# A two-block network in one launch: operands of the first mix in PSUM, scores of the other sign, and GpSimd's weight parts in four pieces

## The chip, the cores and the metric

The kernel runs on one core of one Trainium2 chip. The metric is the device time of one execution in microseconds, as the median of several. The core has a matmul engine (PE), a vector engine (DVE), a scalar engine (ACT), a general engine (GpSimd, POOL in the rows) and a queue engine for transfers (SP).

## The reference, cut to what matters

Two blocks are computed on 256 tokens of width 1024, in float32. The change lies almost wholly in the first mix of the first block:

```python
h = rmsnorm(x, norm1_g[l])
z = h @ w_in[l] + b_in[l]
glu_val, glu_gate, q, k, v, g_conv, g_attn = jnp.split(z, [c0, c1, c2, c3, c4, c5], axis=-1)
conv_out = conformer_conv(glu_val, glu_gate, conv_w[l], conv_b[l], conv_ln_g[l], conv_ln_b[l], w_conv_out[l])
q = rope(q.reshape(B, S, N_Q_HEADS, HEAD_DIM), positions)
k = rope(k.reshape(B, S, N_KV_HEADS, HEAD_DIM), positions)
attn_out = swa_sink_attention(q, k, v, attn_sinks[l]) @ w_attn_o[l]
merged = jax.nn.sigmoid(g_conv) * conv_out + jax.nn.sigmoid(g_attn) * attn_out
x = x + merged @ w_out[l]
```

`conformer_conv` gates, runs a 31-tap convolution over the tokens for each of the 1024 channels, normalises each token over its channels (layernorm), applies SiLU and multiplies by `w_conv_out`. `swa_sink_attention` is attention in a window of 128 tokens over 16 heads, with one learned sink score per head in the softmax (`m = maximum(max(s), sk)`, `e = exp(s - m)`, `p = e / (sum(e) + exp(sk - m))`). Behind it come an expert layer (a projection to keys, a top-16 choice on DVE, gathered rows) and the second block with two mixes and two feed-forward layers.

## The kernel before, in words

Features lie on the 128 partitions and tokens along the free axis, so an activation of one 128-feature chunk is a 128x256 tile. Weights come in tiles of 128x1024, eight blocks of 128x128 each, 279 tiles in all, through a ring of `raw`, `whi` and `wlo` buffers that SP's queue fills. `split_tile` (line 143) makes two parts of a tile: ACT rounds it to `whi` (line 148), and the rest, `wlo = raw - whi`, is made by GpSimd for the 62 tiles in the table `POOL` (line 150) and by DVE for the others (line 152). The 62 are tiles 4 to 51 of the first mix and 14 of the expert layer's 16 query tiles. One output chunk of 128 features is eight blocks with three matmuls each: the high part times the high and the low part of the input, and the low part times the high one (lines 171 to 173). It gathers in a PSUM buffer named `mm`, of which there are four; everything else in PSUM uses four buffers named `ax`.

The first mix is written as a run of chunks, with a `tick` after each one that starts work noted for later (`later(n, fn)`), and a `pump` that issues steps of the convolution until a budget is spent. In order:

- the squares of x are summed (`squares`), `rsqrt` (line 350) makes the scale of each token on DVE with small steps on two columns (lines 357 to 363), and `rows` (line 369) spreads it over all partitions: DVE multiplies the unit matrix by the scale (`dg`, line 373), PE multiplies by ones, ACT copies the result. `normalise` (line 550) forms `h` in SBUF and splits it into `hh` and `hl` (ACT, then DVE's subtraction at line 382). The first four chunks run in fp32 on x before that;
- sixteen chunks make the gated input `u` of the convolution (`gated`); `tables` makes the cosine and sine tables `ct` and `st` on DVE (lines 564 to 582);
- two chunks make keys and values, eight the queries. `rot` (line 676) takes a projection out of PSUM on ACT as `q0`; a chunk later PE swaps the halves (`sw`), and DVE forms `sw*st`, `q0*ct` and their sum (lines 684 to 686);
- sixteen chunks make the two gates. Beside them runs the attention, two heads at a time (`window_pair`): scores on PE, then `soft` (line 713): DVE adds the mask and takes the largest (line 718), changes its sign (line 719), ACT takes the exponentials, DVE forms the reciprocal of the sum, ACT scales; PE transposes and multiplies by the values;
- the convolution has 31 taps for each of eight chunks, two chunks in turn in one `ax` buffer, a DVE step each (line 622); six taps of the last chunk are done by PE. `BUDGET` sets how much of it is issued after each chunk. When `LN0` projections have been issued, the rest is issued, and `mean` (line 758) sums the eight chunks on DVE (`ysum`, lines 760 and 762); PE spreads the mean (line 768), DVE subtracts it, squares are summed, `rsqrt` and `rows` follow, and `silu` gives the input of `w_conv_out`;
- eight chunks each with `w_attn_o`, `w_conv_out` and `w_out` (`residual`, whose low part is made on DVE at line 411).

`rsqrt` and `rows` are also used by all later norms. Line numbers are those of the kernel before; in rows of the changed kernel they are 5 to 8 higher. A scheduler decides the order on each engine from the order of the code; each engine then works through its own instructions in that order and waits where an input is not there.

## Time and profile before

| what | value |
|---|---|
| median of three runs | 1598.98 us (1590.4 to 1600.01) |
| the profiled execution | 1596.75 us, its span 1595.0 us |
| busy over the span: PE, DVE, ACT, GpSimd | 1525.9, 1150.4, 641.4, 512.7 us |
| the first mix's last chunks end, the expert layer's queries begin | about 284 us |
| granted clock of PE, mean | 0.983 |

PE's busy time counts a matmul from its issue to its result, so a busy PE is not always one at its full pace. The first mix takes the first 284 us of the span; from about 400 us on transfers of gathered rows fill the DMA engines.

### The profile page before, as it was taken

To read this page: it belongs to the slowest core of one execution; us is meant where nothing else is said; L and a number is where in the kernel's file an instruction comes from. 1 tells how busy PE (TensorE), PEld (TensorE's weight loads), DVE (VectorE), ACT (ScalarE), POOL (GpSimd) and SP (SyncE) were. 2 spreads that over 40 slices of the span, in tenths; PEclk is the share of its full clock that TensorE was granted. 3 is DMA by queue.
4 is the path that set the end of the run, shared out by engine and by line. 5 is a ranking of instruction groups with operands and counts; after the bars stand their busy time and mean duration, and the time that the engine had idled before them with its cause. 6 is when DMAs were issued, how large, how long until landed. Compare 5 with 4: busy or idle time off the path is not lost.

```text
span 1595.0 us, 29881 instructions
## 1 busy us (share of the span) xinstructions
PE 1525.9 (96%) x11514; PEld 1462.2 (92%) x11514; DVE 1150.4 (72%) x2535; ACT 641.4 (40%) x1378; POOL 512.7 (32%) x407
## 2 busy tenths in 40 slices
PE   8988989889999999799999999999999999999997
PEld 7877889889999999799989999888999998899986
DVE  6998888697989999744444438867777557776655
ACT  4566655442145544000000015556544445655443
POOL 3734541442477787555545501000000030000000
PEclk9999999999999999899999999999999999999999
DMA  5533446746999999999999966734755576465563
GB/s 190 164 101 94 124 130 212 255 157 209 409 409 409 409 409 409 391 408 409 409 409 409 409 232 187 245 120 130 223 185 185 184 193 205 134 192 183 177 190 111
DMA packets 109678, 399.16 MB, mean 250 GB/s; under 512 B 12516, under 2 KB 12931, under 8 KB 109024
## 3 DMA queue, kind: packets, MB, share of 16 engines
q1 hardware_dynamic: 72720, 262.18, 47.9%
q0 software_dynamic: 35232, 130.64, 21.4%
q10 hardware_dynamic: 1584, 4.45, 0.8%
q8 instruction: 90, 1.47, 0.4%
q14 instruction: 52, 0.43, 0.1%
HBM read 395.04 MB, written 6.11 MB: 252 GB/s over the span
## 4 chain that ended last, share of the span: by engine, by line
PE 65%; DMA 17%; DVE 11%; issue 4%; ACT 2%; POOL 1%; SPq 0%; POOLq 0%; DVEq 0%; ACTq 0%
PE mm L1046 17%; DMA row<-vv,idx 14%; PE mm L171 11%; PE mm L173 11%; PE mm L172 11%; PE ax L1154 2%; DVE ax L622 2%; PE mm L239 2%; PE mm L237 2%; PE mm L238 2%; DVE wlo L152 1%; PE ax L1084 1%; DMA wlo<-vv 1%; POOL wlo L150 1%; DMA raw<-vv 1%
## 5 line engine op out<-in xcount | busy, mean ns | idle before, releaser
L148 ACT ACTIVATE whi<-raw 128x1024 fp32r<-128x1024 f32 x275 | 290.1, 1058 | 591.8 <-PE ax L1154 281.9
L152 DVE TENSOR_TENSOR wlo<-raw,whi 128x1024 fp32r<-128x1024 f32 x213 | 260.7, 1226 | 117.6 <-ACT whi L148 113.5
L173 PE MATMUL mm<-xgh,wlo 128*128 128x256 f32 x1064 | 303.0, 285 | 8.3 <-POOL wlo L150 7.6
L171 PE MATMUL mm<-xgh,whi 128*128 128x256 f32 x1064 | 305.2, 287 | 0.5 <-ACT whi L148 0.5
L172 PE MATMUL mm<-xgl,whi 128*128 128x256 f32 x1064 | 302.1, 284 | 2.6 <-DVE xgl L411 2.6
L1655 DVE SCALAR_TENSOR_TENSOR acc<-row,w,acc 128x1024 f32<-128x1024 f32 x94 | 120.7, 1284 | 151.7 <-DMA row<-vv,idx 149.8
L173 PEld LDWEIGHTS mm<-xgh,wlo 128*128 128x128 f32 x1064 | 203.1, 191 | 9.6 <-POOL wlo L150 8.6
L172 PEld LDWEIGHTS mm<-xgl,whi 128*128 128x128 f32 x1064 | 203.1, 191 | 3.0 <-DVE xgl L411 2.8
L171 PEld LDWEIGHTS mm<-xgh,whi 128*128 128x128 f32 x1064 | 203.0, 191 | 2.7 <-issue 1.3
L150 POOL TENSOR_TENSOR wlo<-raw,whi 128x1024 fp32r<-128x1024 f32 x62 | 148.7, 2406 | 127.5 <-ACT whi L148 125.8
L1640 POOL DMA_INDIRECT row<-vv,idx x96 | 124.1, 1292 | 97.4 <-DMA row<-vv,idx 66.4
L1154 PE MATMUL ax<-G,raw 128*128 128x160 f32 x816 | 122.5, 303 | 9.0 <-DMA raw<-vv 9.0
L1154 PEld LDWEIGHTS ax<-G,raw 128*128 128x128 f32 x816 | 115.2, 192 | 9.7 <-DMA raw<-vv 9.6
L1640 POOL DMA_INDIRECT row<-un,idx x96 | 110.8, 1154 | 38.7 <-DVE a L1645 18.2
L1645 DVE CUSTOM_DVE_ANT_0 junk<-row,h 128x1024 f32<-128x1024 f32 x96 | 120.1, 1251 | 0.4
L1046 PE MATMUL mm<-hn,raw 128*128 128x160 f32 x768 | 112.6, 300 | 0.0
L172 PE MATMUL mm<-hl,whi 128*128 128x256 f32 x368 | 106.6, 290 | 2.2 <-DVE hl L382 2.1
L1046 PEld LDWEIGHTS mm<-hn,raw 128*128 128x128 f32 x768 | 106.3, 190 | 0.0
L1154 PE MATMUL ax<-G,whi 128*128 128x160 f32 x624 | 95.4, 303 | 5.1 <-DMA whi<-vv 5.1
L622 DVE SCALAR_TENSOR_TENSOR ax<-u,cw,ax 128x256 f32<-128x256 f32 x227 | 97.3, 481 | 0.6
L1154 PEld LDWEIGHTS ax<-G,whi 128*128 128x128 f32 x624 | 89.1, 193 | 6.0 <-DMA whi<-vv 5.9
L1154 PE MATMUL ax<-G,wlo 128*128 128x160 f32 x608 | 90.2, 300 | 3.1 <-DMA wlo<-vv 3.1
(436 smaller groups left out, 3345.8 us busy)
## 6 DMA issues: line engine op xcount, KB each, us to landing
raw<-wst SPq DMA_DIRECT2D x278, 512.0 KB
raw<-ut SPq DMA_DIRECT2D x48, 512.0 KB
raw<-vv SPq DMA_DIRECT2D x38, 512.0 KB
whi<-ut SPq DMA_DIRECT2D x36, 512.0 KB
wlo<-ut SPq DMA_DIRECT2D x36, 512.0 KB
whi<-vv SPq DMA_DIRECT2D x33, 512.0 KB
wlo<-vv SPq DMA_DIRECT2D x26, 512.0 KB
raw<-vv POOLq DMA_DIRECT2D x13, 512.0 KB
```

Source lines behind the costliest of these rows:

```text
L148: nc.scalar.activation(hi, raw, AF.Copy)
L150: nc.gpsimd.tensor_sub(lo, raw, hi)
L152: self.pin = nc.vector.tensor_sub(lo, raw, hi)
L171: nc.tensor.matmul(pt, w[:, s], xs[0][:, k], start=first, stop=False)
L172: nc.tensor.matmul(pt, w[:, s], xs[1][:, k], start=False, stop=False)
L173: nc.tensor.matmul(pt, lo[:, s], xs[0][:, k], start=False, stop=last)
L622: nc.vector.scalar_tensor_tensor(y[:, c] if k == 30 else ps, u[:, c, k:k + T], cw[:, c, k:k + 1], ps, op0=ALU.mult, op1=ALU.add)
L1046: nc.tensor.matmul(pt, raw[:, k * 128:(k + 1) * 128], hn[:, k, :N], start=(k == 0), stop=(k == C - 1))
L1154: nc.tensor.matmul(acc[d // 2][:, d % 2, :N], raw[:, d * 128:(d + 1) * 128], G(i), start=False, stop=False, skip_group_check=True)
L1640: self.k.nc.gpsimd.indirect_dma_start(t, None, table, bass.IndirectOffsetOnAxis(ap=self.idx[:, s:s + 1], axis=0))
L1645: self.k.nc.vector.tensor_tensor_reduce(junk, row, self.h, 1.0, 0.0, ALU.mult, ALU.add, self.a[:, s:s + 1])
L1655: self.k.nc.vector.scalar_tensor_tensor(self.acc, row, w, self.acc, op0=ALU.mult, op1=ALU.add)
```

## The change

- `BUDGET` and `LN0`: more convolution steps after each chunk of the first stages (4.0 and 2.8 instead of 3.6 and 2.4; a step of a pair counts 0.8), and the layernorm's sum two projections earlier.
- `split_tile`: GpSimd's subtraction of a tile is written as four of 256 columns.
- `rsqrt`: its two small temporaries lie in one `ax` buffer in PSUM, in every norm.
- `rows`: the scaled unit matrix is made by two ACT instructions instead of one of DVE, in every norm.
- the sinks change their sign once at the start; scores are formed with the other sign, so that the smallest is taken and no sign change is left between DVE's and ACT's step; the exponentials scale by -1.
- `normalise`: `h` lies in PSUM.
- `rot`: DVE forms `(pt + bias) * ct` straight from the projection in PSUM, ahead of the swap; the product with `st` stays in PSUM, and the sum reads it there.
- `mean`: the running sum lies in PSUM.

```diff
-BUDGET = (3.6, 2.4, 2.8, 2.6)
+BUDGET = (4.0, 2.8, 2.8, 2.6)
-LN0 = 42
+LN0 = 40
+PIECE = 256
@@ split_tile
-            nc.gpsimd.tensor_sub(lo, raw, hi)
+            for c in range(0, 1024, PIECE):
+                p = slice(c, c + PIECE)
+                nc.gpsimd.tensor_sub(lo[:, p], raw[:, p], hi[:, p])
@@ rsqrt
-        v = self.small.tile([128, n], F32, name="rv", bufs=2)
-        t = self.small.tile([128, n], F32, name="rt", bufs=2)
+        v = self.pp.tile([128, 2 * n], F32, name="ax", bufs=4)
+        v, t = v[:, :n], v[:, n:]
@@ rows
-        nc.vector.tensor_mul(dg, self.ident[:, None, :].to_broadcast([128, 2, 128]),
-                             r[:, :, None].to_broadcast([128, 2, 128]))
+        for tt in range(2):
+            nc.scalar.activation(dg[:, tt], self.ident, AF.Copy, scale=r[:, tt:tt + 1])
@@ first_mix
+        nc.vector.tensor_scalar(snks, snks, -1.0, None, op0=ALU.mult)
@@ normalise
-                h = p1.tile([128, T], F32, name="h", bufs=2)
+                h = self.pp.tile([128, T], F32, name="ax", bufs=4)
@@ rot
+            q1 = p1.tile([128, T], F32, name="q1", bufs=3)
+            nc.vector.scalar_tensor_tensor(q1, pt, bias, ct, op0=ALU.add, op1=ALU.mult)
-                q1 = p1.tile([128, T], F32, name="q1", bufs=2)
-                nc.vector.tensor_mul(q1, sw, st)
-                nc.vector.tensor_mul(q0, q0, ct)
-                nc.vector.tensor_add(dst, q0, q1)
+                nc.vector.tensor_mul(sw, sw, st)
+                nc.vector.tensor_add(dst, sw, q1)
@@ soft
-                    nc.vector.tensor_tensor_reduce(e[:, ks], sp[:, ks], swa[:, ks], 0.125, snk[:, tt:tt + 1], ALU.add, ALU.max, mx[:, tt:tt + 1])
-                nc.vector.tensor_scalar(mx, mx, -1.0, None, op0=ALU.mult)
+                    nc.vector.tensor_tensor_reduce(e[:, ks], sp[:, ks], swa[:, ks], -0.125, snk[:, tt:tt + 1], ALU.add, ALU.min, mx[:, tt:tt + 1])
-                    nc.scalar.activation(e[:, ks], e[:, ks], AF.Exp, bias=mx[:, tt:tt + 1], accum_out=den[:, tt:tt + 1])
-                    nc.scalar.activation(ds[:, tt:tt + 1], snk[:, tt:tt + 1], AF.Exp, bias=mx[:, tt:tt + 1])
+                    nc.scalar.activation(e[:, ks], e[:, ks], AF.Exp, bias=mx[:, tt:tt + 1], scale=-1.0, accum_out=den[:, tt:tt + 1])
+                    nc.scalar.activation(ds[:, tt:tt + 1], snk[:, tt:tt + 1], AF.Exp, bias=mx[:, tt:tt + 1], scale=-1.0)
@@ mean
-            nc.vector.tensor_add(ysum, y[:, 0], y[:, 1])
+            ps = self.pp.tile([128, T], F32, name="ax", bufs=4)
+            nc.vector.tensor_add(ps, y[:, 0], y[:, 1])
             for c in range(2, C):
-                nc.vector.tensor_add(ysum, ysum, y[:, c])
+                nc.vector.tensor_add(ysum if c == C - 1 else ps, ps, y[:, c])
```

DVE's instructions around the first rotation, that of the keys, before the change (`u` is the gated input, `ax<-u,cw,ax` a convolution step):

```order
L642 SCALAR_TENSOR_TENSOR u<-mm,prm,sg 128x256
L622 SCALAR_TENSOR_TENSOR ax<-u,cw,ax 128x256 x11
L684 TENSOR_TENSOR q_817<-ax,st 128x256
L622 SCALAR_TENSOR_TENSOR ax<-u,cw,ax 128x256
L685 TENSOR_TENSOR q_781<-q_781,ct 128x256
L622 SCALAR_TENSOR_TENSOR ax<-u,cw,ax 128x256
L686 TENSOR_TENSOR kT<-q_781,q_817 128x256
L622 SCALAR_TENSOR_TENSOR ax<-u,cw,ax 128x256 x9
```

And the same place on DVE in the changed kernel:

```order
L650 SCALAR_TENSOR_TENSOR u<-mm,prm,sg 128x256
L630 SCALAR_TENSOR_TENSOR ax<-u,cw,ax 128x256 x5
L688 SCALAR_TENSOR_TENSOR q_831<-mm,prm,ct 128x256
L630 SCALAR_TENSOR_TENSOR ax<-u,cw,ax 128x256 x3
L693 TENSOR_TENSOR ax<-ax,st 128x256
L630 SCALAR_TENSOR_TENSOR ax<-u,cw,ax 128x256
L694 TENSOR_TENSOR kT<-ax,q_831 128x256
L630 SCALAR_TENSOR_TENSOR ax<-u,cw,ax 128x256 x7
```

The product with the cosine stands four steps ahead of the one with the sine and reads the projection's `mm` buffer; the last two steps have an operand in `ax`.

DVE's instructions at the end of the convolution before the change (`sga<-sga,mm` takes up a chunk of `w_attn_o`, `y<-ax,y` subtracts the mean):

```order
L622 SCALAR_TENSOR_TENSOR ax<-u,cw,ax 128x256
L815 SCALAR_TENSOR_TENSOR sga<-sga,mm 128x256
L622 SCALAR_TENSOR_TENSOR y<-u,cw,ax 128x256
L815 SCALAR_TENSOR_TENSOR sga<-sga,mm 128x256
L762 TENSOR_TENSOR ysum<-ysum,y 128x256 x2
L815 SCALAR_TENSOR_TENSOR sga<-sga,mm 128x256
L770 SCALAR_TENSOR_TENSOR y<-ax,y 128x256 x4
```

And in the changed kernel:

```order
L823 SCALAR_TENSOR_TENSOR sga<-sga,mm 128x256
L630 SCALAR_TENSOR_TENSOR ax<-u,cw,ax 128x256 x2
L630 SCALAR_TENSOR_TENSOR y<-u,cw,ax 128x256
L770 TENSOR_TENSOR ax<-ax,y 128x256
L770 TENSOR_TENSOR ysum<-ax,y 128x256
L823 SCALAR_TENSOR_TENSOR sga<-sga,mm 128x256
L778 SCALAR_TENSOR_TENSOR y<-ax,y 128x256 x4
```

Before, three chunks of `w_attn_o` are taken up ahead of the subtraction of the mean; in the changed kernel there are four, two of them above the rows shown. On PE the mean's matmul stands behind 73 matmuls of `w_attn_o` before and behind 99 now, of 192.

## Rows read from the trace of the kernel before

**Rows 1.** Busy time per stage: stretch, length, engines, granted clock, DMA share, GB/s.

```profile
core 0: us, PE busy (x) PEld busy (x) DVE busy (x) ACT busy (x) POOL busy (x), PEclk, DMA share, GB/s
60.00:80.00 20.00, 20.00 (x170) 19.95 (x169) 19.12 (x46) 9.24 (x12) 17.57 (x8) 1.00 0.64 202
28.50:73.00 44.50, 38.61 (x302) 37.26 (x301) 43.09 (x87) 23.66 (x30) 31.05 (x14) 0.96 0.49 156
73.00:98.00 25.00, 21.48 (x154) 20.04 (x154) 22.77 (x53) 11.09 (x23) 13.97 (x6) 0.86 0.47 148
98.00:184.00 86.00, 79.82 (x564) 66.57 (x561) 76.93 (x229) 61.86 (x177) 38.34 (x16) 0.96 0.30 93
184.00:206.80 22.80, 21.37 (x182) 21.17 (x181) 22.77 (x50) 10.29 (x13) 17.29 (x8) 1.00 0.53 162
206.80:230.80 24.00, 18.51 (x134) 18.09 (x135) 20.85 (x43) 11.44 (x22) 11.56 (x5) 0.86 0.43 132
230.80:284.00 53.20, 50.44 (x422) 49.85 (x421) 42.19 (x72) 29.35 (x50) 8.78 (x6) 1.00 0.63 200
284.00:346.00 62.00, 53.90 (x429) 52.54 (x428) 50.55 (x248) 27.00 (x62) 33.10 (x29) 0.94 0.63 219
```

**Rows 2.** DVE's groups by form, 0 to 290 us: busy us, mean ns, idle before.

```profile
L622 DVE SCALAR_TENSOR_TENSOR ax<-u,cw,ax 128x256 f32<-128x256 f32 x227 | 97.3, 481 | 0.6
...
L719 DVE TENSOR_SCALAR mx<-mx 128x2 f32<-128x2 f32 x16 | 9.7, 603 | 0.0
L411 DVE SCALAR_TENSOR_TENSOR xgl<-x,prm,xgh 128x256 fp32r<-128x256 f32 x8 | 9.3, 1168 | 2.1 <-ACT xgh L410 2.1
L686 DVE TENSOR_TENSOR qT<-q,q 128x256 f32<-128x256 f32 x8 | 9.2, 1154 | 0.0
L382 DVE TENSOR_TENSOR hl<-h,hh 128x256 fp32r<-128x256 f32 x8 | 8.8, 1139 | 0.0
L685 DVE TENSOR_TENSOR q<-q,ct 128x256 f32<-128x256 f32 x9 | 8.8, 974 | 0.0
...
L762 DVE TENSOR_TENSOR ysum<-ysum,y 128x256 f32<-128x256 f32 x6 | 6.6, 1094 | 0.0
...
L684 DVE TENSOR_TENSOR q<-ax,st 128x256 f32<-128x256 f32 x9 | 3.7, 416 | 1.9 <-PE ax L682 1.9
```

**Rows 3.** GpSimd's timeline, 28 to 62 us: start, length, what.

```profile
37.19 2.39 POOL L150 TENSOR_TENSOR wlo<-raw,whi 128x1024 fp32r<-128x1024 f32 x1 [4.25 <-ACT whi L148]
...
43.94 2.39 POOL L150 TENSOR_TENSOR wlo<-raw,whi 128x1024 fp32r<-128x1024 f32 x1 [0.34 <-ACT whi L148]
52.00 11.83 POOL L150 TENSOR_TENSOR wlo<-raw,whi 128x1024 fp32r<-128x1024 f32 x5 [5.67 <-ACT whi L148]
```

**Rows 4.** DVE's timeline, 36 to 57 us.

```profile
37.36 2.37 DVE L576 TENSOR_SCALAR tb<-tb 128x256 f32<-128x256 f32 x1
...
44.06 2.42 DVE L579 TENSOR_SCALAR tb<-tb 128x256 f32<-128x256 f32 x1
...
52.69 4.41 DVE L622 SCALAR_TENSOR_TENSOR ax<-u,cw,ax 128x256 f32<-128x256 f32 x10
```

**Rows 5.** PE's timeline at the layernorm's scale rows; in brackets idle before and releaser.

```profile
225.04 1.22 PE L376 MATMUL ax<-dg,ones 128*128 128x256 f32 x2 [5.47 <-DVE dg L373]
```

**Rows 6.** DVE's timeline between the mean and the layernorm's scale.

```profile
211.56 2.43 DVE L330 TENSOR_TENSOR sqy<-sqy,sqyq 128x256 f32<-128x256 f32 x1 [0.28 <-ACT sqyq L328]
...
216.84 1.71 DVE L358 TENSOR_SCALAR rr<-rv 128x2 int32<-128x2 int32 x1
218.59 4.58 DVE L362 SCALAR_TENSOR_TENSOR rt<-rv,rr 128x1 f32<-128x1 f32 x2
```

**Rows 7.** Line 362 over the whole span: ns min/median/max, first and last start.

```profile
L362 DVE SCALAR_TENSOR_TENSOR rt<-rv,rr x66: 206/213/2372, 14.7 to 1403.1; 128x1 f32<-128x1 f32 x66
```

**Rows 8.** DVE's groups by form, 284 to 400 us.

```profile
L895 DVE TENSOR_TENSOR cd<-tv 128x48 f32<-128x48 f32 x14 | 12.0, 860 | 0.0
```

**Rows 9.** GpSimd's groups by form, whole span.

```profile
L150 POOL TENSOR_TENSOR wlo<-raw,whi 128x1024 fp32r<-128x1024 f32 x62 | 148.7, 2406 | 127.5 <-ACT whi L148 125.8 <-PE ax L710 1.7
...
L1074 POOL TENSOR_TENSOR R<-QO,gTl 128x512 f16<-128x512 f16 x40 | 67.8, 1696 | 27.6 <-DVE QO L1070 25.4 <-issue 1.8
```

## The prediction

> **What bounds the kernel now.** I read the windows by stage first, then the DVE groups of the first 290 us, then the timelines of the places where the two disagree. Later stages are left aside: the change touches them only in the norm steps.
>
> The windows [rows 1] show the first mix and the start of the expert stage. From 28.5 to 206.8 us DVE is the fullest engine (43.1 of 44.5, 22.8 of 25.0, 76.9 of 86.0, 22.8 of 22.8 us), while PE has slack. PE's own pace is in the first row: 170 matmuls in 20.0 us at granted clock 1.00, 0.1176 us each, so a chunk of 24 takes 2.82 us. By this pace PE needs 302 x 0.1176 = 35.5 us of the 44.5 in the second row: 9.0 us lost. The same count gives 1.4 us for 184 to 206.8, 8.2 for 206.8 to 230.8 and 3.6 for 230.8 to 284. For 73 to 98 and 98 to 184, where longer fp32 matmuls are mixed in, I take the idle time by busy time, 3.5 and 6.2 us, and likewise 8.1 for 284 to 346. Together 40 us: what a faster DVE can give at most at the pace shown.
>
> The DVE groups [rows 2] show where DVE's time goes. L622, the convolution step with one operand in PSUM, takes 481 ns in the mean of 227. Additions and products of the same 128x256 size take 416 to 419 ns in L684 (one operand in PSUM), but 1139 in L382 `hl<-h,hh`, 1154 in L686, 974 in L685, 1094 in L762, all with both operands in SBUF; L719 takes 603 ns for two elements per partition. The timelines of GpSimd and DVE [rows 3, 4] say why. GpSimd subtracts from 37.19 to 39.58 us; DVE's L576 begins at 37.36 and ends at 39.73. The next GpSimd piece at 43.94 is met by L579 at 44.06, which ends at 46.48. From 52.00 to 63.83 us GpSimd works without a break, and ten L622 inside that time take 4.41 us together, no more than elsewhere. So some DVE instructions stand still until GpSimd's 2.4 us operation is over; those with an operand in PSUM do not.
>
> **The change part by part.** Excess of the DVE groups [rows 2], each count times (mean less about 0.42):
> - L719 goes whole (scores of the other sign make it needless): 9.7 us.
> - L686 now adds an operand in PSUM: 8 x 0.73 = 5.9 us.
> - L685 becomes a step of L622's form, 0.48 (L688 of the changed kernel): 9 x 0.49 = 4.4 us, and moves ahead of the swap matmul, off the chain to qT.
> - L382 on `h`: 8 x 0.72 = 5.8 us. L762: 6 x 0.67 = 4.0 us.
>
> That is 30 us of DVE work before 206.8 us, where DVE was busy 165.6 of 178.3 us [rows 1]. The tables' three steps keep two-sided waits but now meet pieces: L576 and L579 fall from about 2.4 us to at most one piece and themselves, about 1 us each; with L578 between them, counted the same, that is some 4 us more [rows 4].
>
> How much of the 34 us shows? Only what PE can use.
> - 28.5 to 73 us: DVE saves L382's and the tables' waits, about 10 us, against 9.0 us of PE slack. I take 7.
> - 73 to 98: L685 and L686 there, against 3.5 us of slack: 3.
> - 98 to 184: of the 20 us of L719, L686 and L685 above, most is freed here, of DVE's 76.9, but PE is idle only 6.2 and ACT is busy 61.9 [rows 1] in the chain scores, exponentials, transposes. I take 5.
> - 184 to 206.8: the convolution's tail, DVE full, PE lost 1.4. As the tail starts earlier, 1.
> - 206.8 to 230.8: PE stands 5.47 us until `dg` [rows 5], and its clock is 0.86 in this stretch [rows 1]. On DVE the chain holds L330 at 2.43, L358 at 1.71 and the pair of L362 at 4.58 us [rows 6]. Undisturbed, L362 takes 0.21, the median of its 66 [rows 7], so the pair 0.43; L358, two elements too, I take at the same 0.21, and L330 at L684's 0.42. That is 7.7 us less, of which L330 may keep a piece. By its order PE has 119 chunk matmuls, 14.0 us, behind the mean's, in the 24.0. The mean's matmul moves one chunk later in that order, so 95 of them, 11.2 us, are left against a chain of about 16.5. The gap falls from 10 to 5.3, by 4.7: I take 5.
> - 230.8 to 284: L411 keeps both operands in SBUF and waits at most one piece instead of 2.4 us; of 8 x 0.75 = 6.0 us half goes, PE idles 3.6: 1.5.
> - 284 to 346: L895, 48 elements, takes 860 ns [rows 8] where 256 take 0.42 undisturbed (L684); pieces cut the 14 x 0.6 to about half, and in GpSimd's queue the parts of the weights stand behind `tops`, which waits for DVE. Of PE's 8.1 us I take 2.5.
>
> Sum 25 us. Against it: at the start DVE gets a product of the sinks that waits for their DMA; behind it on DVE stand the sums of the squares and `h0`, which PE's first chunks need. The DMA is the fifth of six that GpSimd issues there, and DVE waits for `xt` until about the same time; from 0 to 1 us, taken as 0.5. The scale rows are two ACT steps instead of one DVE step; no row here shows them at this place, so from -0.4 (DVE freed) to +1.0 each time that the norm is waited for; 0.5 in the first norm, nothing in the others, where chunks lie between the scale and its use. The operands in PSUM take a buffer of the four that scores and transposes use; from 0 to 2 us in all, taken as 0, since they are held for a few steps only, and the one of the sum is taken when attention is nearly done. Behind a stalled rotation step (L688 reads the projection's bank, which ACT alone released before) PE's next chunk would wait: hidden while DVE is less than three chunks late.
>
> The budgets put ten convolution steps instead of nine between two chunks at first, and the mean two projections earlier; they add no instruction, and what they bring is in the places above.
>
> GpSimd's own cost: 62 operations of 2406 ns [rows 9] become 248. A quarter is 0.60 us; the nearest row that says otherwise is L1074, 1696 ns for 512 elements, 0.85 for 256. I take 0.65 to 0.70, 2.6 to 2.8 us a tile, which is just under PE's 2.82. So nothing is added, but the cover is thin: at 0.85 a tile takes 3.4 us, 0.58 more than PE's chunk.
>
> [...] No row here shows so short an f32 operation. [...]
>
> 25 less 1 is 24. The profiled execution took 1596.75 us (span 1595.0), 2.2 under the median of 1598.98: 1596.75 - 24 is about **1573 us**.
>
> **Rivals.**
> 1. The wait only changes its name. In 73 to 184 us each pair goes PE, DVE, ACT, DVE, ACT, PE, with four buffers; ACT is 72% busy, and L688 now ties PE's banks to DVE. Then those stages give nothing, and half of the others comes: 3.5 + 3 + 1.5 + 1 = 9, so 1588 us. For it: PE already looks busy 79.8 of 86.0 there. Against: DVE was the fullest engine in every stage, and the freed 30 us are no estimate.
> 2. GpSimd sets the pace (slower side). Place: the chunk runs of 28.5 to 73, 184 to 222 and 284 to 346 us, about 38 tiles. Price: four times the piece less 2.82 us for each. At 0.85 us a piece that is 22 us, so 1595, no change. It beats the gain of 24 from (2.82 + 24/38)/4 = 0.86 us on, and the result is slower by over 1% from 0.97 us; at 1.0 us it would be 1618. For it: GpSimd is busy 17.6 of 20.0 us at full pace [rows 1]. Against: no row has so short an f32 operation above 0.85.
> 3. All of PE's slack goes, and the clock, at 0.86 in two stages, stays up: 40 us and a little, 1555. For it: DVE's load falls under PE's in every stage. Against: the norm chains remain.
> 4. The operands in PSUM change nothing, since what waits is the result's place. Then only L719 and the pieces help: about 10 us, 1587. Against it: L622 with its result in PSUM and GpSimd at work [rows 3, 4].
>
> **How the numbers follow.** Chances: the forecast (saves 16 to 34) 0.58; rival 3 0.17; rival 1 0.13; rival 4 0.02; GpSimd's pace 0.10, of which half ends within 1% and half slower. About 1% (16 us) is what a measurement of this kernel can tell from no change, so faster means under 1583. Faster 0.58 + 0.17 = 0.75; same 0.13 + 0.02 + 0.05 = 0.20; slower 0.05. The range runs from just under rival 3 to just past rival 1: 1552 to 1592; it leaves out GpSimd's slower half and half of rival 3's tail.
>
> **What would show it.** Right: the new rotation steps at 0.42 to 0.48 us, no DVE step of these lines above 0.5; L576, L578 and L579 and L411 at about one piece more than alone; pieces of 0.6 to 0.7 us; the matmul on `ysum` near 186 us instead of 206.8; the wait before `dg` shorter than 5.5 us; the first mix's last chunk some 20 us earlier, with everything behind it shifted by the same amount. Wrong: pieces over 0.8 us and PE waiting for `wlo` through 50 to 73 us; ACT idle less but PE's span from 98 to 184 unchanged; DVE idle where it was full, with PE waiting on `ax` buffers.

## The result, and the profile after

| | median us | ratio to before, 95% interval |
|---|---|---|
| before (four runs now) | 1598.47 | |
| after | 1574.03 | 0.9864, 0.9844 to 0.9884 |
| after, in a later comparison (before 1596.84) | 1577.37 | 0.9873, 0.9847 to 0.9898 |

The forecast was 1573.0 us, faster. The total came out; the way to it did not, as the experiments show: three parts of the change, tried by themselves, save about 37 us (e11), and two others give some 13 to 15 of it back.

The windows of after, with the edges of [rows 1] (work that stood in one of them before now lies earlier). In rows of after, L150 is ACT's rounding to `whi` and L155 GpSimd's subtraction:

```profile
core 0: us, PE busy (x) PEld busy (x) DVE busy (x) ACT busy (x) POOL busy (x), PEclk, DMA share, GB/s
60.00:80.00 20.00, 20.00 (x166) 19.42 (x165) 17.59 (x48) 10.09 (x15) 20.00 (x30) 1.00 0.57 186
28.50:73.00 44.50, 43.57 (x357) 42.90 (x356) 41.40 (x101) 26.88 (x34) 39.46 (x56) 1.00 0.57 182
73.00:98.00 25.00, 24.93 (x183) 22.26 (x182) 23.28 (x72) 19.53 (x50) 18.74 (x28) 1.00 0.45 144
98.00:184.00 86.00, 86.00 (x687) 77.62 (x686) 74.72 (x230) 62.74 (x161) 61.05 (x88) 1.00 0.43 135
184.00:206.80 22.80, 17.11 (x112) 16.24 (x111) 16.69 (x44) 14.54 (x32) 11.88 (x16) 0.81 0.44 137
206.80:230.80 24.00, 24.00 (x200) 23.91 (x200) 18.29 (x34) 11.42 (x17) 0.00 (x0) 0.97 0.50 154
230.80:284.00 53.20, 44.86 (x344) 43.65 (x343) 33.56 (x83) 23.23 (x44) 24.76 (x33) 0.94 0.71 252
284.00:346.00 62.00, 62.00 (x502) 61.64 (x501) 57.38 (x306) 26.96 (x63) 27.65 (x49) 1.00 0.41 142
```

PE is all but full from 28.5 to 184 us at granted clock 1.00, where before it had 0.96, 0.86 and 0.96. DVE is no longer the fullest engine in any stretch there. GpSimd now works without a break from 60 to 80 us, 20.00 us against 17.57.

DVE's groups by form, 0 to 290 us, of after (busy us, mean ns, idle before), to be read against [rows 2]:

```profile
L732 DVE TENSOR_TENSOR den<-den,ds 128x2 f32<-128x2 f32 x16 | 5.4, 334 | 0.2 <-ACT ds L731 0.2
L417 DVE SCALAR_TENSOR_TENSOR xgl<-x,prm,xgh 128x256 fp32r<-128x256 f32 x8 | 4.7, 590 | 2.5 <-ACT xgh L416 2.5
...
L688 DVE SCALAR_TENSOR_TENSOR q<-mm,prm,ct 128x256 f32<-128x256 f32 x9 | 4.3, 477 | 1.2 <-ACT q L686 1.2
...
L694 DVE TENSOR_TENSOR qT<-ax,q 128x256 f32<-128x256 f32 x8 | 3.3, 417 | 0.0
...
L388 DVE TENSOR_TENSOR hl<-ax,hh 128x256 fp32r<-128x256 f32 x8 | 2.9, 416 | 0.0
```

The steps with an operand in PSUM stand at their own length: `qT` 417 ns for 1154, `hl` 416 for 1139, the product with `ct` 477 for 974. Two steps with all operands in SBUF are shorter by the pieces alone: L417 590 for 1168 (1169 in e2, with whole tiles), L732 334 for e2's 578. A result in PSUM is not enough: of the eight steps of L561, which read two tiles in SBUF and write `h` to PSUM, the median takes 492 ns, but the longest, beside GpSimd's first pieces, 966.

GpSimd's part, and what PE waited for in 0 to 290 us of after (total us, times, longest):

```profile
L155 POOL TENSOR_TENSOR wlo<-raw,whi x248: 720/737/1708, 21.9 to 314.0; 128x256 fp32r<-128x256 f32 x124
```

```profile
PE ax L382 <- ACT dg L380: 4.5, 1, 4.5
PE mm L178 <- DVE wlo L157: 3.7, 1, 3.7
PE mm L176 <- ACT yhl L387: 3.6, 1, 3.6
...
PE mm L178 <- POOL wlo L155: 0.5, 1, 0.5
```

A piece takes 737 ns in the median (minimum 720, longest 1708). PE's matmuls wait only 0.5 us for GpSimd, its weight loads 1.9. Before, from 284 to 346 us, GpSimd was what PE waited for most:

```profile
PE mm L173 <- POOL wlo L150: 7.6, 5, 2.0
```

In that window e1 and after have no such wait. PE's longest wait in after is one that the kernel before did not have at that place: for the scale rows that ACT now makes.

First starts on PE in us, of the profiled executions of before, after and the kernels below that matter most. The last column is the end less the last mark:

| kernel | mean (`ysum`) | `w_conv_out` | first query chunk | last score with keys | first 128x512 matmul behind the expert layer | end | rest |
|---|---|---|---|---|---|---|---|
| before | 206.8 | 230.4 | 276.7 | 344.9 | 1017.7 | 1595.0 | 577.3 |
| after | 182.6 | 202.6 | 251.7 | 317.7 | 990.8 | 1570.7 | 579.9 |
| e1 | 198.5 | 220.9 | 267.2 | 326.9 | 1000.2 | 1576.2 | 576.0 |
| e7 | 193.8 | 211.6 | 261.9 | 321.8 | 994.5 | 1570.7 | 576.2 |
| e11 | 181.4 | 203.8 | 249.9 | 310.4 | 983.4 | 1559.4 | 576.0 |
| e9 | 184.5 | 201.1 | 249.8 | 310.9 | 983.8 | 1560.2 | 576.4 |
| e6 | 184.1 | 200.7 | 249.4 | 314.3 | 990.9 | 1567.2 | 576.3 |
| e10 | 195.0 | 211.5 | 260.3 | 325.5 | 1002.2 | 1581.8 | 579.6 |

After leads by 27.8 us at `w_conv_out` (230.4 - 202.6), 25.0 at the first query chunk, 26.9 behind the expert layer and 24.3 at the end: it gains more than the forecast says in the first mix and loses some behind it. The stretch between the last score and the 128x512 matmul can't carry a reading of a few us: it takes 672.7 to 677.0 us over all profiles, and after's two differ by 3.9 (673.1 and 677.0).

### The profile page after: what moved, and what is told of

It is laid out like the page before. It is cut to its first block, busy times and chain, and to the rows that moved or that the text cites. A ratio compares the mean times of both kernels' runs of the same rounds, so it can differ in the third digit from the quotient of the medians.

```text
span 1570.7 us, 30113 instructions
## 1 busy us (share of the span) xinstructions
PE 1520.5 (97%) x11514; PEld 1462.8 (93%) x11514; DVE 1111.3 (71%) x2510; ACT 647.5 (41%) x1398; POOL 546.5 (35%) x593
## 4 chain that ended last, share of the span: by engine, by line
PE 81%; DMA 10%; DVE 4%; issue 2%; POOL 1%; ACT 1%; ACTq 0%; POOLq 0%; DVEq 0%
PE mm L1054 17%; PE mm L176 14%; PE mm L178 13%; PE mm L177 13%; PE ax L1162 12%; DMA row<-vv,idx 3%; DMA whi<-vv 2%; DMA raw<-wst 2%; PE mm L244 2%; PE mm L243 2%; PE mm L242 2%; POOL wlo L155 1%; PE ax L1092 1%; DMA wlo<-vv 1%; DVE wlo L157 1%
## 5 line engine op out<-in xcount | busy, mean ns | idle before, releaser
L150 ACT ACTIVATE whi<-raw 128x1024 fp32r<-128x1024 f32 x275 | 290.5, 1059 | 604.4 <-PE ax L1162 281.9
L157 DVE TENSOR_TENSOR wlo<-raw,whi 128x1024 fp32r<-128x1024 f32 x213 | 262.5, 1235 | 115.0 <-ACT whi L150 110.9
L178 PE MATMUL mm<-xgh,wlo 128*128 128x256 f32 x1064 | 302.5, 284 | 3.7 <-DVE wlo L157 3.7
L178 PEld LDWEIGHTS mm<-xgh,wlo 128*128 128x128 f32 x1064 | 204.9, 193 | 4.3 <-DVE wlo L157 3.9
L155 POOL TENSOR_TENSOR wlo<-raw,whi 128x256 fp32r<-128x256 f32 x248 | 180.4, 762 | 80.7 <-ACT whi L150 80.4
```

The lines of the kernel that those rows point to most:

```text
L150: nc.scalar.activation(hi, raw, AF.Copy)
L155: nc.gpsimd.tensor_sub(lo[:, p], raw[:, p], hi[:, p])
L157: self.pin = nc.vector.tensor_sub(lo, raw, hi)
L178: nc.tensor.matmul(pt, lo[:, s], xs[0][:, k], start=False, stop=last)
```

## The experiments

Medians and ratios are against before in the same comparison. Line numbers shift from kernel to kernel: the product with the cosine, L685 before, is L687 in e1 and L693 in e10; the change of sign, L719 before, is L721 in e7.

**e1: the four pieces alone**, in the kernel before.

```diff
-            nc.gpsimd.tensor_sub(lo, raw, hi)
+            for c in range(0, 1024, 256):
+                p = slice(c, c + 256)
+                nc.gpsimd.tensor_sub(lo[:, p], raw[:, p], hi[:, p])
```

> The kernel before with GpSimd's subtraction in four pieces and nothing else. Theory (DVE steps with two SBUF operands stand still for what is left of GpSimd's running instruction, and pieces bound that to 0.74 us): the mean of L686, L685, L382 on h and L762 falls from about 1.1 us to 0.6 to 0.7, DVE is freed of some 15 to 20 us, 8 to 13 us show, 1586 to 1591 us. Rival A (only the operands in PSUM matter; pieces cost GpSimd 0.54 us a tile and bring nothing): those lines stay near 1.1 us, 1598 to 1603. Rival B (the pieces are the whole of it): 1574 to 1577.

Measured 1578.85 us, ratio 0.9892 (0.9868 to 0.9917). That is far more than the prediction had given to the pieces, and next to the range of rival B, the pieces as the whole of the gain. Part of it may not go by DVE's waits at all: the stretch from the first query chunk to the last score got 8.5 us shorter (68.2 to 59.7 in the table), and PE's waits for `wlo` there, 7.6 us before, are gone. A quarter of a tile is ready sooner than a whole one (0.74 us for 2.41), and DVE's steps of that stretch got shorter too (those of L895 271 ns in the mean from 276 to 346 us, before 1226); no run separates the two. It still has one large wait. GpSimd's timeline (start, length), DVE's, and PE's waits from 60 to 120 us:

```profile
46.64 38.98 POOL L152 TENSOR_TENSOR wlo<-raw,whi 128x256 fp32r<-128x256 f32 x56 [1.48 <-PE mm L174]
```

```profile
71.43 14.47 DVE L687 TENSOR_TENSOR q<-q,ct 128x256 f32<-128x256 f32 x1
```

```profile
PE ax L712 <- DVE qT L688: 12.4, 1, 12.4
```

One product of two tiles in SBUF begins while GpSimd works through 56 pieces without a break, and ends at 85.90, just after GpSimd's last piece at 85.62: it stands behind the last 20 or so (14.47 us at 0.70 each). All of DVE stands behind it, and PE waits 12.4 us.

**e2: everything but the pieces**, in after.

```diff
-PIECE = 256
+PIECE = 1024
```

> The changed kernel with GpSimd's subtraction whole again (128x1024, about 2.4 us). Theory: the steps that moved to PSUM stay at 0.42 to 0.48 us, while those that kept two SBUF operands (L417, L732, L335, L582, L903) wait up to 2.4 us again, some 8 to 12 us of DVE, of which half shows; GpSimd gives 0.5 us a tile back: 1575 to 1580. Rival (GpSimd's 2.95 us a tile is what now paces the chunks): 1566 to 1571, faster than the changed kernel. Rival B (pieces are the whole of the gain): 1593 to 1600.

Measured 1590.04, ratio 0.9954 (0.994 to 0.9968): 10 us and more above the theory's range, and just under that of rival B. It is the cleanest test of the operand in PSUM: beside whole tiles the subtraction that now reads `h` from PSUM takes its own length, 415 ns (four of the eight from 25.74 to 27.15 us, beside the tile that GpSimd begins at 25.4), where it took 1139, while L417, untouched by the change, stays at 1169.

```profile
L388 DVE TENSOR_TENSOR hl<-ax,hh 128x256 fp32r<-128x256 f32 x8 | 2.9, 415 | 0.0
```

The total hides what these parts are worth, since e2 also holds the two that cost. In its profiled execution (1594.93 us) it leads before by 14.9 us at the first matmul of `w_attn_o`, which stands behind all attention (181.75 against 196.64), and by 2.7 at the end (1592.3 against 1595.0). The windows of e1, and then of e2, show where pieces and operands work:

```profile
28.50:73.00 44.50, 43.43 (x359) 42.68 (x359) 43.93 (x101) 26.41 (x34) 41.07 (x58) 1.00 0.56 181
73.00:98.00 25.00, 12.64 (x89) 11.58 (x88) 24.29 (x38) 8.36 (x19) 12.62 (x19) 0.73 0.39 125
98.00:184.00 86.00, 84.22 (x626) 71.60 (x626) 78.39 (x248) 65.38 (x181) 50.10 (x70) 1.00 0.32 100
```

```profile
28.50:73.00 44.50, 41.26 (x309) 40.54 (x308) 40.34 (x92) 26.63 (x35) 31.28 (x13) 0.92 0.55 177
73.00:98.00 25.00, 25.00 (x202) 23.61 (x201) 22.09 (x66) 16.84 (x43) 15.81 (x7) 1.00 0.41 131
98.00:184.00 86.00, 83.94 (x646) 73.83 (x644) 78.63 (x232) 64.30 (x170) 47.10 (x21) 1.00 0.39 124
```

Up to 73 us the pieces bring 57 matmuls (359 for 302) and the rest of the change 7. From 73 to 184 us it is the other way: e2 has 848 for 718, and e1, which loses 12.4 us to its stand, 715.

**e3: the old budgets**, in after.

```diff
-BUDGET = (4.0, 2.8, 2.8, 2.6)
+BUDGET = (3.6, 2.4, 2.8, 2.6)
...
-LN0 = 40
+LN0 = 42
```

> The changed kernel with BUDGET (3.6, 2.4, 2.8, 2.6) and LN0 42 as before. Theory (the gain is DVE's freed time, the order only follows): the same within 3 us, 1572 to 1577, the mean's matmul at 183 to 187 us. Rival (the earlier convolution and mean bring the gap before the layernorm down): 1579 to 1585, with the stand of PE before the w_conv_out chunks back at 8 to 10 us.

Measured 1576.37, ratio 0.9873 (0.9847 to 0.9899), the same as after. The budgets bring nothing that can be measured.

**e4: the scale rows by DVE**, as before, in after.

```diff
-        for tt in range(2):
-            nc.scalar.activation(dg[:, tt], self.ident, AF.Copy, scale=r[:, tt:tt + 1])
+        nc.vector.tensor_mul(dg, self.ident[:, None, :].to_broadcast([128, 2, 128]),
+                             r[:, :, None].to_broadcast([128, 2, 128]))
```

> The changed kernel with dg made by one DVE product as before, in every norm. Theory (ACT's two steps stand behind the queue of eight row transfers that ACT issues at 253 to 264 us, and behind roundings of weights in the later norms, which cost 1.7 to 4 us of the second block): 1570 to 1573. Rival (PE is stopped there by its four full mm buffers in any case): 1574 plus or minus 1, with PE's stand between 255 and 266 us unchanged.

Measured 1572.96, ratio 0.985 (0.9823 to 0.9877). The total is in the theory's range, but its interval can't be told from after's. Two places moved against each other: the first query chunk came at 255.0 instead of 251.7, the last score at 315.7 instead of 317.7. The stretch between them fell from 66.0 to 60.7 us.

**e5: pieces of 512**, in after.

```diff
-PIECE = 256
+PIECE = 512
```

> After, with GpSimd's pieces of 512 elements instead of 256. From the two lengths measured (0.737 us for 256, 2.406 for 1024) a piece of 512 is estimated at 1.29 us and a tile at 2.59 instead of 2.95. Theory (what counts is how long a DVE step with both operands in SBUF stands behind GpSimd): a third of the way from pieces of 256 (1574) to whole tiles (1590), so 1577 to 1582, and L732, L417 and L947 between their means of the two. Rival (GpSimd's pace counts, as a tile in four pieces takes longer than PE's 2.82 us): 1569 to 1573, and PE's matmuls from 60 to 80 us back at 170 from 166.

Measured 1582.71, ratio 0.99 (0.9875 to 0.9925), a piece 1292 ns in the median. The time lies between whole tiles and quarters, just above the theory's range; the faster tile (2 x 1.29 us for 4 x 0.74) helps nothing, and PE's matmuls from 60 to 80 us are 166 as in after. The length of the piece counts, not GpSimd's pace; it counts for PE too, which waits 4.1 us for `wlo` over the span, against 0.5 in after and 8.3 in e2.

**e6: the square root's temporaries in SBUF**, in after.

```diff
-        v = self.pp.tile([128, 2 * n], F32, name="ax", bufs=4)
-        v, t = v[:, :n], v[:, n:]
+        v = self.small.tile([128, n], F32, name="rv", bufs=2)
+        t = self.small.tile([128, n], F32, name="rt", bufs=2)
```

> After, with the temporaries of the reciprocal square root back in SBUF for every norm. After loses about 3 us of its lead from 1000 us on (from there to the end 579.9 us against 577.3 before). Theory (those temporaries hold one of the four PSUM buffers while the gate's norm of the odd mix is worked out, and PE's L1520 stands for it): 1571 to 1573, and from the first chunk of the down projection to the end 577 to 578.5. Rival (the loss comes with the scale rows by ACT, or with where the tiles lie): 1574 to 1576, the second half as long as in after, and the first mix up to 1 us longer.

Measured 1568.06, ratio 0.9812 (0.9787 to 0.9838), below the theory's range: the rest takes 576.3 us, and the first query chunk comes 2.3 us earlier too. The effect is there; the reason in the expectation is not the one in the trace. DVE's timeline at the gate's norm, of after:

```profile
1305.03 0.16 DVE L363 TENSOR_SCALAR ax<-st 128x1 f32<-128x1 f32 x1
...
1307.56 0.23 DVE L368 SCALAR_TENSOR_TENSOR ax<-ax,rr 128x1 f32<-128x1 f32 x1
1307.68 0.69 DVE L1487 TENSOR_TENSOR bias<-bias,na 128x512 f32<-128x512 f32 x1
1308.29 0.23 DVE L368 SCALAR_TENSOR_TENSOR ax<-ax,rr 128x1 f32<-128x1 f32 x1
...
1314.72 0.89 DVE L1514 TENSOR_SCALAR vz<-vz,rr 128x512 f32<-128x512 f32 x2
```

and the same place of e6:

```profile
1302.63 0.25 DVE L363 TENSOR_SCALAR rv<-st 128x1 f32<-128x1 f32 x2
...
1304.38 0.35 DVE L368 SCALAR_TENSOR_TENSOR rt<-rv,rr 128x1 f32<-128x1 f32 x2
...
1310.05 0.88 DVE L1514 TENSOR_SCALAR vz<-vz,rr 128x512 f32<-128x512 f32 x2
```

With the temporaries in PSUM the order on DVE sets a step of 0.69 us between the two small steps of a pair; in SBUF the pair stands together. The chain from L363 to the scaling takes 9.69 us (1314.72 - 1305.03) against 7.42 (1310.05 - 1302.63). What PE's sequencer waits for at the gate's matmuls (ns: shortest, median, longest), of after and then of e6:

```profile
L1520 PEldq EVENT_SEMAPHORE  x3: 51/51/3940, 1311.2 to 1315.3; - x3
```

```profile
L1520 PEldq EVENT_SEMAPHORE  x3: 51/51/1060, 1309.4 to 1310.6; - x3
```

2.9 us of the 3.6 by which the rest differs (579.9 - 576.3) lie here; the runs show no place for the other 0.7. In all seven profiles with the temporaries of these norms in PSUM the rest takes 579.4 to 580.9 us, in the seven with them in SBUF 575.7 to 577.3.

**e7: the pieces and the rotations**; of the change nothing else, so e1 with:

```diff
+            q1 = p1.tile([128, T], F32, name="q1", bufs=3)
+            nc.vector.scalar_tensor_tensor(q1, pt, bias, ct, op0=ALU.add, op1=ALU.mult)
...
-                q1 = p1.tile([128, T], F32, name="q1", bufs=2)
-                nc.vector.tensor_mul(q1, sw, st)
-                nc.vector.tensor_mul(q0, q0, ct)
-                nc.vector.tensor_add(dst, q0, q1)
+                nc.vector.tensor_mul(sw, sw, st)
+                nc.vector.tensor_add(dst, sw, q1)
```

> Before with the four pieces and the rotation steps with an operand in PSUM, and nothing else of the change. In the run with pieces alone one rotation step (L687) stood 14.47 us behind 37 pieces, and PE 12.4 us for qT. Theory (that stand is what pieces alone lacked most): the step is gone, 1571 to 1575, and the mean's matmul at 184 to 190 us instead of 198.5. Rival (the stand was hidden or is made up elsewhere, and the rest of the change is needed): 1576 to 1580, mean's matmul not before 194 us.

Measured 1573.75, ratio 0.9849 (0.983 to 0.9869). The total is the theory's and the stand of the product is gone, but the mean's matmul at 193.8 is next to the rival's 194. (The 37 pieces of the expectation are some 20, as said at e1.) GpSimd's and DVE's timelines and PE's waits show a second stand of the same kind:

```profile
47.73 39.03 POOL L152 TENSOR_TENSOR wlo<-raw,whi 128x256 fp32r<-128x256 f32 x56 [1.48 <-PE mm L174]
```

```profile
81.99 4.80 DVE L721 TENSOR_SCALAR mx<-mx 128x2 f32<-128x2 f32 x1
```

```profile
PE ax L686 <- ACT q L680: 4.1, 1, 4.1
```

The change of sign of two columns meets the run of 56 pieces that ends at 86.76 (47.73 + 39.03) and itself ends at 86.79. ACT's exponentials wait for it, the projection that PE's swap needs stands behind them on ACT, and PE waits 4.1 us.

**e8: the square root in PSUM and the rows by ACT in the first mix's two norms only**, the other norms as before. Both get a switch, which those two calls turn on:

```diff
-    def rsqrt(self, r, pt, width, eps=EPS):
+    def rsqrt(self, r, pt, width, eps=EPS, psum=False):
...
-    def rows(self, r, dst):
+    def rows(self, r, dst, act=False):
...
-                self.rsqrt(r, sums, D)
-                self.rows(r, rb)
+                self.rsqrt(r, sums, D, psum=True)
+                self.rows(r, rb, act=True)
...
-            self.rsqrt(rv, sums, D)
+            self.rsqrt(rv, sums, D, psum=True)
...
-            self.rows(rv, rl)
+            self.rows(rv, rl, act=True)
```

> After, with the square root's temporaries in PSUM and the scale rows by ACT only in the first mix's two norms (input and layernorm); in all other norms both are as before. Scale rows by DVE everywhere shortened the query stage by 5.3 us (66.0 to 60.7) but came 3 us later to the products (93.6 against 90.6). Theory (both hold, and the two places are apart): query stage 60 to 62 us long, products at 90 to 91 us, second half 577 to 578.5 us, in all 1564 to 1569. Rival (what the query stage gains is given back behind it, as PE waits for the weights' parts there anyway): 1571 to 1575.

Measured 1565.24, ratio 0.9786 (0.977 to 0.9803). The stretch of the queries takes 62.2 us (252.6 to 314.8), the rest 575.7: both gains are there together.

**e9: e6 with the rows by ACT only in those two norms.**

```diff
-    def rows(self, r, dst):
+    def rows(self, r, dst, act=False):
...
-                self.rows(r, rb)
+                self.rows(r, rb, act=True)
...
-            self.rows(rv, rl)
+            self.rows(rv, rl, act=True)
```

> After, with the square root's temporaries in SBUF for every norm (as in the run rsqrt in SBUF, 1568) and the scale rows by ACT only in the first mix's two norms (as in the run first mix only, 1565). Theory: the second half is 576 us as in both, the query stage about 60 us as in the latter, the layernorm's first chunk at 200 to 201 us as in the former (202.8 with the temporaries in PSUM): 1562 to 1566. Rival (the first mix does not care where those temporaries lie, its chunk at 202 to 203): 1565 to 1568.

Measured 1561.68, ratio 0.9779 (0.9754 to 0.9804), 0.3 us under the theory's range, with the first chunk of `w_conv_out` at 201.1, as the theory has it. By its time alone it can't be told from e8.

**e10: the rotations undone**, in after: the diff of e7 the other way round, its core

```diff
-            nc.vector.scalar_tensor_tensor(q1, pt, bias, ct, op0=ALU.add, op1=ALU.mult)
...
+                nc.vector.tensor_mul(q0, q0, ct)
```

> After, with the rotation steps as before (products of tiles in SBUF, sums of tiles in SBUF). Theory (a DVE step with all its operands in SBUF that meets GpSimd's first long run of pieces stands until the run ends, as L687 did for 14.47 us and L721 for 4.80): the product for kT, due at about 67 us, stands until the run's end at 80 to 83 us, PE waits 8 us or more for it, and the time is 1580 to 1590. Rival (a step stands for one piece, and those two were chance): no DVE step above 2 us, 1575 to 1579.

Measured 1584.58, ratio 0.9924 (0.9896 to 0.9953), in the theory's range. GpSimd, DVE and PE's wait again:

```profile
46.60 38.94 POOL L155 TENSOR_TENSOR wlo<-raw,whi 128x256 fp32r<-128x256 f32 x56 [0.43 <-ACT whi L150]
```

```profile
71.67 14.16 DVE L693 TENSOR_TENSOR q<-q,ct 128x256 f32<-128x256 f32 x1
```

```profile
PE ax L718 <- DVE qT L694: 12.4, 1, 12.4
```

The stand comes back at the same step and again ends with GpSimd's run (85.83 against 85.54). The two stands of e1 and e7 were no chance.

**e11: e7 and the scores of the other sign**; of the change nothing else.

```diff
-                    nc.vector.tensor_tensor_reduce(e[:, ks], sp[:, ks], swa[:, ks], 0.125, snk[:, tt:tt + 1], ALU.add, ALU.max, mx[:, tt:tt + 1])
-                nc.vector.tensor_scalar(mx, mx, -1.0, None, op0=ALU.mult)
+                    nc.vector.tensor_tensor_reduce(e[:, ks], sp[:, ks], swa[:, ks], -0.125, snk[:, tt:tt + 1], ALU.add, ALU.min, mx[:, tt:tt + 1])
...
```

The sinks' change of sign and the scale of the exponentials are those of the change.

> Before with the four pieces, the rotation steps with an operand in PSUM and the scores of the other sign; nothing else. With pieces and rotations alone L721, the step that turns the sign of the maxima, stood 4.80 us and PE 4.14 us at 92 us; its 16 took 11.4 us of DVE. Theory (that stand and DVE's 11 us are what that run lacked in the attention stage): PE's wait of 4.14 us is gone, the mean's matmul comes 4 to 8 us earlier than its 193.8, and the time is 1565 to 1571. Rival (DVE has slack there by now): 1572 to 1576.

Measured 1560.68, ratio 0.9768 (0.9743 to 0.9792): better than the theory's range. The windows of e7, and then of e11:

```profile
73.00:98.00 25.00, 20.86 (x145) 18.62 (x145) 22.86 (x61) 14.41 (x37) 18.39 (x27) 0.87 0.42 133
98.00:184.00 86.00, 85.34 (x643) 74.52 (x643) 79.03 (x244) 63.85 (x171) 51.91 (x75) 1.00 0.37 116
```

```profile
73.00:98.00 25.00, 25.00 (x193) 23.19 (x191) 23.69 (x74) 19.27 (x50) 19.27 (x29) 1.00 0.53 168
98.00:184.00 86.00, 86.00 (x691) 77.70 (x690) 77.45 (x238) 64.38 (x166) 62.82 (x89) 1.00 0.43 130
```

By this count half of what the sign brings lies at the stand (48 matmuls more from 73 to 98 us, and the clock at 1.00 instead of 0.87), half in the attention behind it (48 more from 98 to 184); at the 0.1176 us of a matmul at full pace the 96 are 11.3 us, and the mean's matmul moved by 12.4.

**e12: after once more.**

> The changed kernel once more, beside the three others on one chip, as the reference for differences of a few us: 1572 to 1577, with the second half about 580 us long and PE's wait of 4.5 us behind the scale rows at 265 us, as in its first profile; if either is absent, the runs that undo them showed chance.

Measured 1577.37, 0.4 us above the upper edge; its rest takes 580.1 us (1575.7 - 995.6), and PE waits 4.88 us for the rows at 267 us. So what e6, e8 and e9 undo was no accident of one run.

Side by side, with the saving worked out as (1 - ratio) x 1597 us:

| kernel | saves, us |
|---|---|
| pieces (e1) | 17 |
| pieces, rotations (e7) | 24 |
| pieces, rotations, sign (e11) | 37 |
| these, `h` and the running sum in PSUM, budgets, rows by ACT in two norms (e9) | 35 |
| these, rows by ACT in all norms (e6) | 30 |
| these, square root in PSUM (after) | 22, 20 |
| after without rotations (e10) | 12 |
| after without pieces (e2) | 7 |

The intervals of e7 and e11 are apart (0.983 to 0.9869, 0.9743 to 0.9792), those of e6 and after just so (0.9787 to 0.9838, 0.9844 to 0.9884), those of the first run of after and e10 too; e12 and e10 touch, but in their one comparison the slowest of after took 1577.74 us and the fastest of e10 1581.53. Those of e1 and e7 touch; e11 and e9 can't be told apart, nor, by their times alone, e9 and e6. Both e11 and e9 beat after.

## Why the prediction was right, and where its steps failed

- **The mechanism held.** DVE steps that had no operand in PSUM stood while GpSimd worked and, given one, no longer do (L382 on `h` 1139 ns before, 415 in e2 with the same whole tiles). New rotation steps at 0.42 to 0.48 us as forecast; the mean at 182.6 against 186; PE all but full in 28.5 to 184 us. Rival 4 (operands in PSUM change nothing) falls by e2, where steps that only read PSUM have their own length beside whole tiles (`hl` 415 ns, `qT` 416), and by e10, where a product out of SBUF stands 14.16 us; L622, which the prediction holds against it, does not tell, as its result lies in PSUM as well. Rival 1 falls by the windows, rival 2 by e5 and the 0.5 us that PE waits for `wlo`.
- **Stage by stage the sum did not come.** Lead of after over before, forecast and measured: at the first matmul of `w_attn_o` 14 (7 + 3 + 5 less 1) and 25.7 us (196.64 to 170.97); at `w_conv_out` 20 and 27.8; at the first query chunk 21.5 and 25.0; at the end 24 and 24.3. The term that was far too small is that of the attention. In the two windows from 73 to 184 us PE does 870 matmuls for 718, 152 more, which are 17.9 us at 0.1176; the prediction took 8, as it read 9.7 us of slack there (3.5 + 6.2) from PE's busy time and not from matmuls at full pace. (From 28.5 to 73 us the count comes out: 55 more, 6.5 us, where it took 7.) It also calls DVE the fullest engine from 28.5 to 206.8 us, but from 98 to 184 PE was busier already (79.82 against 76.93). That the total still met the forecast is luck: what was lost behind attention happened to be as large as what was gained too much before it.
- **The forecast of the piece was too low.** "I take 0.65 to 0.70" became 0.737. That is 2.95 us for the four of a tile, a little more than the 2.82 of PE's chunk that 0.70 would have stayed under. No cost of it shows: PE went on at 166 matmuls in 20 us, against 170, and with whole tiles (e2) it has 167.
- **The pieces were worth more than was forecast.** Of the 34 us of DVE work the prediction credits 30 to operands in PSUM and L719 and 4 to the tables' pieces; behind 230.8 us it takes 1.5 and 2.5 us for pieces, and rival 4 puts L719 and the pieces together at "about 10 us". The pieces alone saved 17 us (e1). They bring most of the gain up to 73 us, where quarter tiles shorten the waits of steps without PSUM (L382 on `h` 592 ns in e1 for 1139), and 8.5 us in the query stretch, where the prediction has 2.5 and does not see that PE itself waited 7.6 for whole tiles of GpSimd. In the attention the pieces alone gain nothing, as the stand takes what they save there (715 matmuls for 718), while the operands in PSUM and the sign gain 130 with whole tiles (e2), as the prediction says.
- **A missing term.** The prediction has a step wait "at most one piece". That holds for L417 in after (1.00 us at the longest) and for L732 (0.79), but not in GpSimd's first long run: there a step without PSUM stood 14.47, 14.16 and 4.80 us in three kernels. After escapes because the rotations and the sign leave no such step inside that run (45.90 to 82.08; the next one, L732, begins at 82.42, so the escape is narrow), and therein lies much of their worth: the sign brings 13 us (37 - 24), where the prediction has 5 for a whole stage in which it is one of three parts.
- **Two costs taken as nothing.** For the rows by ACT "nothing in the others, where chunks lie between the scale and its use" fails at the expert layer's norm. ACT's timeline of after:

```profile
253.59 11.02 ACTq L867 DMA_DIRECT2D row<-ut  x6
264.65 0.38 ACT L972 ACTIVATE pq<-mm 128x256 f32<-128x256 f32 x1 [11.13 <-DMA raw<-wst]
264.93 0.68 ACT L380 ACTIVATE dg<-ident,rr 128x128 f32<-128x128 f32 x2
```

  The rows stand in ACT's queue behind transfers that take 11.02 us to issue, and PE waits 4.5 us. DVE's eight steps that need the rows come later for it, a weight part that DVE makes stands behind them, and PE waits another 3.7 us (`PE mm L178 <- DVE wlo L157` above). With the rows by DVE (e9) that second wait is gone, PE waits 0.9 for the rows and 2.2 for `pq`, which stands behind the same issues, and the stretch from the first query chunk to the last score falls from 64.9 us (e6) to 61.1. "From 0 to 2 us in all, taken as 0" for the operands in PSUM fails for the square root, 8 to 10 us by the savings of after and e6. Of these 2.9 are shown, at the gate's norm, by what the place of the temporaries does to the order on DVE; some 2 to 4 lie ahead of the first query chunk (249.4 in e6 for 251.7 and, in e12, 253.3), most of it in the layernorm chain; for what is left the runs show no place.
- **Rival 3 was half the truth.** e11 saves 37 us, near the 40 and "a little" of rival 3, and its clock is 1.00 from 28.5 to 184 us, though 0.85 from there to 206.8. The forecast's sum came true since two parts taken as free cost about what the others brought beyond it.
- **The layernorm chain.** "The gap falls from 10 to 5.3, by 4.7" became a fall of 0.5. By the prediction's own count, from the mean's matmul to the first of `w_conv_out` less 0.1176 us for each chunk matmul between, before has 23.6 us less 119 matmuls, a gap of 9.6, and after 20.0 less 93 (the prediction has 95), a gap of 9.1: a wait for `yhl` of 3.6 us takes the place of the one for `dg`. In e6 and e9, with the square root's temporaries in SBUF, it is 16.6 us less 96 matmuls, the forecast's 5.3. Their place is not all that decides it: e3, with them in PSUM and the old budgets, has 16.2 less 96, a gap of 5.0. The granted clock there, in windows of after run again (e12) and then of e6:

```profile
192.00:196.00 4.00, 4.00 (x23) 4.00 (x24) 1.64 (x9) 0.00 (x0) 2.47 (x4) 0.60 0.59 147
...
204.00:208.00 4.00, 3.44 (x14) 3.14 (x15) 3.48 (x8) 4.00 (x12) 0.00 (x0) 0.50 0.37 122
```

```profile
192.00:196.00 4.00, 3.23 (x27) 3.02 (x26) 3.69 (x12) 0.00 (x0) 2.97 (x5) 1.00 0.47 133
...
204.00:208.00 4.00, 4.00 (x37) 4.00 (x36) 3.63 (x9) 3.44 (x7) 0.00 (x0) 1.00 0.03 11
```

  After (e12) idles 1.53 us, then 3.61, and is granted 0.60 and 0.50 behind them. E6 idles 0.56, 1.70, 0.46 and 2.21 us and stays at 1.00. Why there is a fall behind 1.53 us and none behind 1.70, the runs don't show.

## What to carry to other kernels

Where a trace shows steps of one engine standing beside another (here 1139 ns for 415), shorten the pieces of the other first (592 ns in e1), and then look for the last steps that still meet a long run of pieces: one such step made PE wait 12.4 us (e1, e10). Shorter pieces can also bring the first part of a result sooner to an engine that waits for it (here 0.74 us for 2.41): look whether it waited. Where the slack of an engine sets a bound, count its instructions at full pace, not its busy time. Try the parts of a change in a growing chain, each kernel one part more than the last; a total that fits a forecast can hide two errors of opposite sign. Before a small step goes to another engine, read what stands in that engine's queue, its DMA issues included, and look at the order that the scheduler makes of the steps that were only given another place.

## What the runs showed of the hardware that was not expected

A DVE step without PSUM operands got in between GpSimd's pieces at some places, and at others not at all. In after, from 267 us on, eight such steps and GpSimd's pieces pass each other one by one:

```profile
267.18 10.05 POOL L155 TENSOR_TENSOR wlo<-raw,whi 128x256 fp32r<-128x256 f32 x11 [10.31 <-ACT whi L150]
```

```profile
267.41 6.88 DVE L947 SCALAR_TENSOR_TENSOR hn<-x,prm,rb 128x256 f32<-128x256 f32 x8 [9.45 <-ACT rb L383]
```

0.86 us a step (0.48 in before, where GpSimd stands idle beside it) and 0.91 us a piece, so each waits for the other. In the runs of 56 pieces of e1, e7 and e10 a piece follows the last in 0.70 us (38.98 / 56) and the step waits for the end. With whole tiles [rows 6] two steps in 4.58 us got in behind a tile each. What decides between the two was not tried and stays open.
